# A mixture-of-experts kernel: first gather ahead of two weight loads, first tables ahead of the splits, the overflow branch behind the last expert

## The chip, the cores and the metric

The kernel runs on one core of a Trainium2 chip. The metric is the device time of one execution in microseconds, as the median of several runs. Beside those runs there is one profiled execution, with a trace of every instruction. All times of the trace count from the start of its span. The engines are PE (TensorE: matmuls and transposes), DVE (VectorE), ACT (ScalarE), POOL (GpSimd) and SP (SyncE, which here only issues DMAs). Each engine runs its own list of instructions strictly in that list's order.

## What is computed

The reference is a model of two layers on 512 tokens of width 1024. The part that this case is about is the mixture of experts at the end of the first layer: a router picks 4 of 32 experts for each token, and each expert is a clamped SwiGLU.

```python
def moe(h, w_router, b_router, w_gu, b_gu, w_down, b_down):
    """Top-4-of-32 clamped SwiGLU experts; tokens sorted by expert into expert-homogeneous blocks."""
    ...
    logits = (xt @ w_router + b_router).astype(jnp.float32)
    top_vals, top_idx = lax.top_k(logits, TOP_K)
    ...
```

An expert's gate and up weights are 1024 x 2048 and its down weights 1024 x 1024, all float32. The first layer's mixer (gated linear attention and pooling) runs ahead of this, and the second layer follows it: a short Fourier mixing of 128 x 256 pieces, attention with keys and values, and a dense feed-forward part.

## The kernel before, in words

`phase_a` is the first layer up to the router. `phase_b` (L1070 on) is the mixture of experts, and `phase_c` the second layer. Only `phase_b` is changed.

**Experts.** Each expert has a block of 96 slots (`SLOTS`). `gather(e)` (L1092) is an indirect DMA that POOL issues: it fetches the 96 token rows of expert e from `h2d`, in DRAM, into `xg`. `turn` (L1098) transposes them on PE (`pxT`) and splits the result into two parts, `xTh` (a rounded copy, on ACT) and `xTl` (the rest, on DVE). `gate_up(e)` (L1123) runs over 8 slabs of 128 x 2048 weights, `swiglu` (L1138) makes `g` and `u` from its PSUM (L1142 to L1145), `turn` makes `aTh` and `aTl` of them, and `down(e)` (L1148) runs over 4 slabs of the down weights and ends in `y` (L1162) and a scatter with accumulation into `ydr` (L1163), again by POOL. In the program `down(e-1)` stands behind `gate_up(e)`, so PE has the down of the expert before to do while `g` and `u` are made.

**Weights.** `W.get` (L204; its work is in `split`, L147 and L148) takes one slab of 1 MB: it is loaded into one of 9 raw buffers, ACT casts it to `whi`, and DVE subtracts to get `wlo`. One slab feeds 12 matmuls with 512 columns: `whi` with the rounded rows, `wlo` with the rounded rows, `whi` with the rest. There are 4 pairs of `whi` and `wlo`. Seven raw slabs are loaded ahead of the mixture of experts through SP's queue and two more (`ahead[SH:AH]`) through POOL's queue. `held` are the first three splits, written ahead of the loop.

**Tables.** `tables(b)` (L933) makes the row numbers, scatter numbers and weights of four experts: four comparisons `oh` on DVE (L940), 16 small matmuls `ptab` (L944), and some ten small operations on DVE. `tables(0)` stands ahead of the loop, and each further one is called in the gate and up part of every fourth expert. The first gather does not need it; it has its numbers `gi0` from the router.

**Further blocks.** `overflows` (L958) counts the blocks beyond the first of each expert and loads the count into a register of every engine. `overflow` (L976) is a branch, `tc.If(n > 0)`, with a loop over such blocks (L983). With the data here no expert has more than 96 rows, and the branch is skipped.

**What sets the order.** The kernel is written as a program in one order, and a scheduler makes of it a list for each engine, ready instructions first as it judges, within the dependences. A branch is a wall for it: nothing is moved across it. In `order`'s rows below a name is the tile that is written, then `<-`, then the tiles that are read.

Of the kernel before, what the change touches and what calls it, by code (L numbers as in the profile page):

```python
# [29 lines left out]
AH, SH, HN = 9, 7, 3  # L30
# [902 lines left out]
def tables(S, pl, bank, b):  # L933

    nc = S.nc
    es = slice(b * 4, b * 4 + 4)
    oh = pl.tile([128, NT, 4, SLOTS], BF, name="oh", tag="oh", bufs=1)
    iota = S.k[:, None, K_IOTA:K_IOTA + SLOTS].to_broadcast([128, 4, SLOTS])
    for i in range(NT):
        nc.vector.tensor_tensor(oh[:, i], iota, S.pos[:, i, es, None].to_broadcast([128, 4, SLOTS]), op=OP.is_equal)  # L940
    p = bank("ptab")
    for e in range(4):
        for i in range(NT):
            nc.tensor.matmul(p[:SLOTS, e * 6:e * 6 + 6], oh[:, i, e, :], S.V[:, i, b * 4 + e, :], start=i == 0, stop=i == NT - 1)  # L944
    sl = pl.tile([SLOTS, 4, 6], F32, name="sl", tag="sl", bufs=2)
    nc.vector.tensor_copy(sl, p[:SLOTS, 0:24].rearrange("p (e c) -> p e c", e=4))
    t = pl.tile([SLOTS, 4, 4], F32, name="tsl", tag="tsl", bufs=2)
    tok, sct = t[:, :, 0], t[:, :, 1]
    nc.vector.tensor_tensor(tok, sl[:, :, 0], sl[:, :, 1], op=OP.add)
    nc.vector.tensor_copy(S.gi[:, es], tok)  # L950

    nc.vector.scalar_tensor_tensor(sct, sl[:, :, 2], S.k[:SLOTS, K_NSLOT:K_NSLOT + 1], tok, op0=OP.mult, op1=OP.add)
    nc.vector.tensor_scalar(S.si[:, es], sct, S.k[:SLOTS, K_SLOT:K_SLOT + 1], None, op0=OP.add)
    nc.vector.tensor_tensor(sct, sl[:, :, 3], sl[:, :, 4], op=OP.add)
    nc.vector.tensor_tensor(S.wt[:, es], sct, sl[:, :, 5], op=OP.add)
# [114 lines left out]
def phase_b(S):  # L1070
    nc, tc, I = S.nc, S.tc, S.I
    mm = nc.tensor.matmul
    with ExitStack() as bx:
# [4 lines left out]
        W = Weights(S, bx, 2048, 9, "b_w", (2, 3, 0, 1, 4, 5, 8, 6, 7))  # L1078
        W.open_parts(bx, 4, "b_wp", (0, 1, 2, 3, 4, 7, 6, 5))
        pl = bx.enter_context(tc.tile_pool(name="b_pool", bufs=1, reuse_waits="tile"))  # L1080
# [11 lines left out]
        def gather(e, gi=None):  # L1092
            xg[e] = pl.tile([SLOTS, D], F32, name="xg", tag="xg", bufs=2)
            gi = S.gi[:, e:e + 1] if gi is None else gi
            S.gathered = nc.gpsimd.indirect_dma_start(out=xg[e], out_offset=None, in_=S.h2d,
                                         in_offset=bass.IndirectOffsetOnAxis(ap=gi, axis=0)).ins

        def turn(src, dst, e, name, bufs, scale=1.0):  # L1098
            dst[e] = [pl.tile([128, KT, SLOTS], F32R, name=name + n, tag=name + n, bufs=bufs) for n in "hl"]
            for h in range(2):  # L1100
                p = bank("p" + name)
                for k in range(4):
                    kk = h * 4 + k
                    nc.tensor.transpose(p[:, k * SLOTS:(k + 1) * SLOTS], src[:, kk * 128:(kk + 1) * 128], S.ident[:SLOTS, :SLOTS])  # L1104
                hi, lo = [t[:, h * 4:h * 4 + 4, :] for t in dst[e]]
                p = p[:, :4 * SLOTS].rearrange("p (k t) -> p k t", k=4)
                if scale == 1.0:
                    split(S, hi, lo, p)
                else:
                    nc.scalar.mul(hi, p, scale)  # L1110
                    nc.vector.scalar_tensor_tensor(lo, p, scale, hi.bitcast(F32), op0=OP.mult, op1=OP.subtract)
# [61 lines left out]
                nc.sync.dma_start(br[64 + h:96 + h, 0:512], bgu[:, 1536:2048])  # L1173
                nc.sync.dma_start(br[64 + h:96 + h, 512:1536], bdn)
        S.ahead = W.last

        with tc.issue_after(S.h2d_last):
            W.ahead(ahead[SH:AH], [128, 2048], nc.gpsimd)
        nc.vector.tensor_copy(sel.rearrange("p h e -> p (h e)"), S.k[:, K_SEL:K_SEL + 64])
        gather(0, S.gi0)  # L1180
        with tc.issue_after(S.gathered):
            nc.gpsimd.dma_start(S.g2b, bcast(S.adr, D, off=3 * D, parts=SLOTS))
        with tc.issue_after(S.gathered):
            overflows(S, pl)
        overflow(S, pl, ps, bank, W)
        held = [W.get(I["w_gu"][0, 0, k * 128:(k + 1) * 128, :], [128, 2048]) for k in range(HN)]
        tables(S, pl, bank, 0)
        gather(1)
        turn(xg.pop(0), xT, 0, "xT", 2)
        for e in range(NE + 1):  # L1190
            if e < NE:
                between = {BK: biases} if e == 0 else {}
                if e % 4 == 0 and e // 4 + 1 < NE // 4:
                    between[TK] = lambda: tables(S, pl, bank, e // 4 + 1)
                if e + 1 < NE:
                    between[XK] = lambda: turn(xg.pop(e + 1), xT, e + 1, "xT", 2)
                p = gate_up(e, between)
                ac[e] = swiglu(e, p)
                if e == 6:
                    vectors(S, pl, bank)  # L1200
                if e + 2 < NE:
                    gather(e + 2)
            if e > 0:
                down(e - 1)
            if e < NE:
                turn(ac.pop(e), aT, e, "aT", 1, 1.0 / ALPHA)


def turned(S, pl, bank, xT, i, xn):
# [710 lines left out]
```

## Time and profile before

| what | value |
|---|---|
| median of 3 runs | 2286.84 us (2286.39 to 2287.12) |
| profiled execution | 2284.15 us |
| its span in the trace | 2282.4 us |
| PE busy | 2163.1 us, 95% of the span |
| DVE busy | 1802.1 us, 79% |
| ACT busy | 1335.7 us, 59% |
| POOL busy | 339.2 us, 15% |
| mean rate of all DMAs | 246 GB/s over the span |

The profiled execution is 2.69 us below the median of the runs, and 1.75 us longer than its span. The share of busy time is an average over stages. The mixture of experts takes the stretch from about 322 us to 1533 us, and the second layer what is behind it. In the rows further down, a number in brackets at a row's end is the time the engine stood idle just ahead of that row, and behind the arrow stands what it waited for.

### The profile page before, as it was taken

Reading aid. Unit: us, or ns where it says so; the run is one execution under the profiler, and the core shown is the slowest. Engines: PE = TensorE matmul, PEld = TensorE weight load, DVE = VectorE, ACT = ScalarE, POOL = GpSimd, SP = SyncE. Lnnn points to the kernel's source line nnn. Section 1 sums busy time; section 2 is a strip of 40 time slices with the busy share of each in tenths; the row PEclk is TensorE's granted clock in tenths of the full one; section 3 lists DMA queues with packets and bytes.
Section 4 is the critical chain, followed back from the end, with each engine's and each line's share of the span. In section 5 each row is a group of like instructions: output and inputs, shape, how many; then the busy total and the mean of one; then the engine's idle time right before and its main releaser. Section 6 shows DMA issues by size and latency. Waiting matters only on the chain.

```text
span 2282.4 us, 27718 instructions
## 1 busy us (share of the span) xinstructions
PE 2163.1 (95%) x10501; PEld 1626.5 (71%) x10501; DVE 1802.1 (79%) x2000; ACT 1335.7 (59%) x1487; POOL 339.2 (15%) x186
## 2 busy tenths in 40 slices
PE   7998879999999999999999999989999999999998
PEld 3787666777766666666666666667777888878776
DVE  3748789999989898988898989876478454689885
ACT  3434346767766666666666667655354443388872
POOL 3202210100112121312221212151000000000000
PEclk9899989999999999999999999999999999999999
DMA  7644568999999999999999999966311234323222
GB/s 256 200 148 135 221 234 314 370 371 364 369 349 350 361 346 368 341 369 347 361 348 363 344 370 354 350 229 223 102 47 53 79 118 139 121 74 92 93 83 93
DMA packets 158049, 561.98 MB, mean 246 GB/s; under 512 B 12964, under 2 KB 55304, under 8 KB 125128
## 3 DMA queue, kind: packets, MB, share of 16 engines
q1 hardware_dynamic: 146880, 522.37, 62.3%
q0 software_dynamic: 9968, 36.10, 5.9%
q10 hardware_dynamic: 1064, 1.70, 0.3%
q8 instruction: 84, 1.38, 0.2%
q14 instruction: 53, 0.43, 0.1%
HBM read 534.94 MB, written 25.58 MB: 246 GB/s over the span
## 4 chain that ended last, share of the span: by engine, by line
PE 80%; DVE 11%; DMA 3%; issue 3%; ACT 2%; POOL 1%; SPq 0%; POOLq 0%; DVEq 0%; ACTq 0%
PE pgu L1132 31%; PE pd L1159 12%; DVE wlo L148 3%; PE pjf L153 3%; PE pjf L155 3%; PE pjf L154 3%; PE pop L155 2%; PE pop L153 2%; PE pop L154 2%; DVE u L1144 1%; PE pgu L1115 1%; PE pada L272 1%; DMA ydr<-y,si 1%; PE pxT L1104 1%; PE paT L1104 1%
## 5 line engine op out<-in xcount | busy, mean ns | idle before, releaser
L148 DVE TENSOR_TENSOR wlo<-raw,whi 128x2048 fp32r<-128x2048 f32 (+2 forms) x498 | 1002.5, 2040 | 102.7 <-ACT whi L147 84.2
L147 ACT CAST whi<-raw 128x2048 fp32r<-128x2048 f32 (+2 forms) x454 | 790.6, 1777 | 180.7 <-PE pgu L1132 85.4
L1163 POOL DMA_INDIRECT ydr<-y,si x32 | 185.6, 5801 | 808.8 <-DVE y L1162 777.4
L1132 PE MATMUL pgu<-whi,xTh 128*96 128x512 f32 x1024 | 281.2, 396 | 2.6 <-DVE u L1144 2.6
L1132 PE MATMUL pgu<-wlo,xTh 128*96 128x512 f32 x1024 | 278.5, 394 | 0.3 <-DVE wlo L148 0.3
L1132 PE MATMUL pgu<-whi,xTl 128*96 128x512 f32 x1024 | 278.5, 394 | 0.0
L1132 PEld LDWEIGHTS pgu<-wlo,xTh 128*96 128x96 f32 x1024 | 165.2, 162 | 70.8 <-DVE wlo L148 0.7
L1132 PEld LDWEIGHTS pgu<-whi,xTl 128*96 128x96 f32 x1024 | 165.3, 162 | 69.8 <-issue 0.5
L1132 PEld LDWEIGHTS pgu<-whi,xTh 128*96 128x96 f32 x1024 | 161.7, 162 | 70.2 <-issue 3.2
L1159 PE MATMUL pd<-wlo,aTh 128*96 128x512 f32 x512 | 162.4, 398 | 32.5 <-DVE wlo L148 32.5
L153 PE MATMUL pjf<-xTh,whi 128*128 128x512 f32 (+1 forms) x480 | 181.7, 379 | 1.5 <-DVE rsq L221 1.5
L155 PE MATMUL pjf<-xTh,wlo 128*128 128x512 f32 (+1 forms) x480 | 180.9, 378 | 2.1 <-DVE wlo L148 2.1
L154 PE MATMUL pjf<-xTl,whi 128*128 128x512 f32 (+1 forms) x480 | 180.5, 376 | 0.0
L1159 PE MATMUL pd<-whi,aTh 128*96 128x512 f32 x512 | 159.6, 393 | 0.0
L1159 PE MATMUL pd<-whi,aTl 128*96 128x512 f32 x512 | 159.3, 392 | 0.0
L1159 PEld LDWEIGHTS pd<-wlo,aTh 128*96 128x96 f32 x512 | 79.0, 161 | 72.3 <-DVE wlo L148 43.2
L1143 ACT ACTIVATE g<-g 96x1024 f32<-96x1024 f32 x32 | 33.9, 1060 | 137.0 <-DVE g L1142 137.0
L1159 PEld LDWEIGHTS pd<-whi,aTl 128*96 128x96 f32 x512 | 82.3, 161 | 35.5
L1159 PEld LDWEIGHTS pd<-whi,aTh 128*96 128x96 f32 x512 | 82.3, 161 | 35.4
L155 PEld LDWEIGHTS pjf<-xTh,wlo 128*128 128x128 f32 x480 | 90.3, 188 | 19.2 <-DVE wlo L148 2.9
L153 PEld LDWEIGHTS pjf<-xTh,whi 128*128 128x128 f32 x480 | 90.4, 188 | 17.8 <-ACT jkr L1485 1.4
L154 PEld LDWEIGHTS pjf<-xTl,whi 128*128 128x128 f32 x480 | 90.4, 188 | 16.3
(541 smaller groups left out, 3542.2 us busy)
## 6 DMA issues: line engine op xcount, KB each, us to landing
raw<-in_w_gu_dram SPq DMA_DIRECT2D x254, 1024.0 KB, 9.2
raw<-in_w_down_dram SPq DMA_DIRECT2D x128, 1024.0 KB, 7.0
raw<-in_w_ada_dram SPq DMA_DIRECT2D x40, 512.0 KB, 4.6
raw<-in_even_w_in_dram SPq DMA_DIRECT2D x36, 512.0 KB, 3.5
raw<-in_odd_w_in_dram SPq DMA_DIRECT2D x32, 512.0 KB, 3.8
raw<-in_even_w_out_dram SPq DMA_DIRECT2D x16, 512.0 KB, 3.3
raw<-in_odd_w_out_dram SPq DMA_DIRECT2D x16, 512.0 KB, 3.1
raw<-in_w_in_dram SPq DMA_DIRECT2D x14, 512.0 KB, 4.7
```

The source lines that it names most:

```text
L147: S.nc.scalar.copy(hi, src)
L148: S.nc.vector.tensor_tensor(lo, src, hi.bitcast(F32), op=OP.subtract)
L153: mm(ps, lh, rh, start=start, stop=False)
L154: mm(ps, lh, rl, start=False, stop=False)
L155: mm(ps, ll, rh, start=False, stop=stop)
L272: mm(p[n][q * 32:(q + 1) * 32, :], ada[:, j, :], w[:, n, :], start=j < 4, stop=j >= 4)
L1104: nc.tensor.transpose(p[:, k * SLOTS:(k + 1) * SLOTS], src[:, kk * 128:(kk + 1) * 128], S.ident[:SLOTS, :SLOTS])
L1115: mm(p[:, c * 512:(c + 1) * 512], lhs, bt[:, b % 3 * 512:(b % 3 + 1) * 512], start=start, stop=stop)
L1132: mm(p[:, c * 512:(c + 1) * 512], a[:, k, :], w[:, c * 512:(c + 1) * 512], start=k == 0 and w is wh and a is xh, stop=False)
L1143: nc.scalar.activation(g, g, AF.Silu, scale=ALPHA)
L1159: mm(p[:, c * 512:(c + 1) * 512], a[:, k0 + k, :], w[:, k, c * 512:(c + 1) * 512], start=False, stop=k0 + k == KT - 1 and a is al)
L1163: nc.gpsimd.indirect_dma_start(out=S.ydr, out_offset=bass.IndirectOffsetOnAxis(ap=S.si[:, e:e + 1], axis=0), in_=y, in_offset=None, comput ...
```

## The change

It has three parts, all in `phase_b`. The first gather is issued by POOL ahead of the two weight loads on POOL's queue, which now wait for it in the order. `tables(0)` is written ahead of the three splits of `held`. `overflow`, with its branch and the pair of weight buffers that it borrows, is written behind the loop over the experts.

```diff
         S.ahead = W.last
-
-        with tc.issue_after(S.h2d_last):
-            W.ahead(ahead[SH:AH], [128, 2048], nc.gpsimd)
         nc.vector.tensor_copy(sel.rearrange("p h e -> p (h e)"), S.k[:, K_SEL:K_SEL + 64])
         gather(0, S.gi0)
+        with tc.issue_after(S.gathered):
+            W.ahead(ahead[SH:AH], [128, 2048], nc.gpsimd)
         with tc.issue_after(S.gathered):
             nc.gpsimd.dma_start(S.g2b, bcast(S.adr, D, off=3 * D, parts=SLOTS))
         with tc.issue_after(S.gathered):
             overflows(S, pl)
-        overflow(S, pl, ps, bank, W)
+        tables(S, pl, bank, 0)
         held = [W.get(I["w_gu"][0, 0, k * 128:(k + 1) * 128, :], [128, 2048]) for k in range(HN)]
-        tables(S, pl, bank, 0)
         gather(1)
         turn(xg.pop(0), xT, 0, "xT", 2)
...
             if e < NE:
                 turn(ac.pop(e), aT, e, "aT", 1, 1.0 / ALPHA)
+        overflow(S, pl, ps, bank, W)
```

The scheduler's lists change with it far beyond these lines. Three places follow.

**DVE at the start.** This is DVE's list behind the small operations of the router, before. `ox` and `oni` belong to `overflows`; L983 is the branch.

```order
L964 SCALAR_TENSOR_TENSOR ox<-cnt,ox 128x32 x4
L966 TENSOR_TENSOR_SCAN ox<-ox 128x32
L968 CAST oni<-ox 1x1
L148 TENSOR_TENSOR wlo<-raw,whi 128x2048 x3
L971 TENSOR_LOAD oni
L983 COMPARE_AND_BRANCH x2
...
L940 TENSOR_TENSOR oh<-cst_k,pos 128x384 x4
L148 TENSOR_TENSOR wlo<-raw,whi 128x2048
L946 COPY sl<-ptab 96x24
L148 TENSOR_TENSOR xTl<-pxT,xTh 128x384
```

And the same place now:

```order
L968 CAST oni<-ox 1x1
L946 COPY sl<-ptab 96x24
L940 TENSOR_TENSOR oh<-cst_k,pos 128x384
L949 TENSOR_TENSOR tsl<-sl 96x4
L940 TENSOR_TENSOR oh<-cst_k,pos 128x384
L950 CAST gi<-tsl 96x4
L952 SCALAR_TENSOR_TENSOR tsl<-sl,cst_k,tsl 96x4
L148 TENSOR_TENSOR xTl<-pxT,xTh 128x384
L953 TENSOR_SCALAR si<-tsl,cst_k 96x4
L148 TENSOR_TENSOR xTl<-pxT,xTh 128x384
L954 TENSOR_TENSOR tsl<-sl 96x4
L940 TENSOR_TENSOR oh<-cst_k,pos 128x384
```

Before, three `wlo` stand ahead of the branch and so ahead of the gathered rows' `xTl`, and a fourth follows ahead of it. Now no `wlo` stands ahead of `xTl`; comparisons of the first and second tables do.

**DVE around expert 4's `g`.** `pd` is the down part of expert 3, and the numbers tell the buffers apart. This is DVE before, and below it now; the `wlo` that expert 3's down reads are 4173, 4191, 4209 and 4227 before, and 4011, 4029, 4047 and 4065 now.

```order
L148 TENSOR_TENSOR wlo_4173<-raw_4170,whi_4172 128x2048
L148 TENSOR_TENSOR xTl_4086<-pxT_4087,xTh_4085 128x384
L148 TENSOR_TENSOR xTl_4086<-pxT_4094,xTh_4085 128x384
...
L148 TENSOR_TENSOR wlo_4191<-raw_4188,whi_4190 128x2048
...
L148 TENSOR_TENSOR wlo_4209<-raw_4206,whi_4208 128x2048
L1142 TENSOR_SCALAR g_4159<-pgu_3963 96x1024
L1144 TENSOR_SCALAR u_4160<-pgu_3963 96x1024
L148 TENSOR_TENSOR wlo_4227<-raw_4224,whi_4226 128x2048
```

```order
L148 TENSOR_TENSOR wlo_3978<-raw_3975,whi_3977 128x2048
L148 TENSOR_TENSOR wlo_4011<-raw_4008,whi_4010 128x2048
L1142 TENSOR_SCALAR g_3997<-pgu_3801 96x1024
L1144 TENSOR_SCALAR u_3998<-pgu_3801 96x1024
L148 TENSOR_TENSOR wlo_4029<-raw_4026,whi_4028 128x2048
L1145 SCALAR_TENSOR_TENSOR u_3998<-u_3998,g_3997 96x1024
L148 TENSOR_TENSOR wlo_4047<-raw_4044,whi_4046 128x2048
```

Before, three of the down part's four `wlo` stand ahead of `g` of expert 4; now one does, and the second stands behind `g` and `u`.

**SP behind the last expert.** Before, the loads for the second layer stand in one row; `fw` are the weights of the Fourier mixing.

```order
L197 DMA raw<-in_cst_dch_dram 128x2x512
L1713 DMA fnw<-in_final_norm_w_dram 128x1024
L1714 DMA env<-in_even_norm_dram 128x1024
L1353 DMA fw<-in_fourier_w_dram 128x4x256 x2
L197 DMA raw<-in_even_w_in_dram 128x2x512 x4
L1726 DMA hr<-ydr 128x1024 x4
```

Now (between the two pieces lies the body of the branch, which is skipped):

```order
L1713 DMA env<-in_even_norm_dram 128x1024
L197 DMA raw<-in_even_w_in_dram 128x2x512 x3
L971 TENSOR_LOAD oni
L983 COMPARE_AND_BRANCH x2
...
L1352 DMA fw<-in_fourier_w_dram 128x4x256 x2
L197 DMA raw<-in_even_w_in_dram 128x2x512
L1725 DMA hr<-ydr 128x1024 x4
```

The two loads of `fw` moved behind three of the four `raw` loads and behind the branch. On PE, 95 of the 96 matmuls `pG` that read `fw`'s split stood ahead of the first transposes of the second layer's rows (`pxn`) before, and 55 do now.

## Rows read from the trace of the kernel before

**Rows 1.** The page's part 5: busy time, mean ns, idle before and releaser.

```profile
L1159 PE MATMUL pd<-wlo,aTh 128*96 128x512 f32 x512 | 162.4, 398 | 32.5 <-DVE wlo L148 32.5
```

**Rows 2.** Busy time by stretch, from one expert's g to the next.

```profile
core 0: us, PE busy (x) PEld busy (x) DVE busy (x) ACT busy (x) POOL busy (x), PEclk, DMA share, GB/s
361.66:390.86 29.20, 26.70 (x119) 18.89 (x120) 25.39 (x21) 19.06 (x15) 1.34 (x1) 0.94 0.89 338
...
462.21:498.91 36.70, 36.70 (x184) 26.22 (x183) 35.66 (x33) 25.58 (x18) 3.13 (x2) 1.00 1.01 373
498.91:534.72 35.81, 35.81 (x168) 25.40 (x167) 33.50 (x22) 25.49 (x18) 2.85 (x2) 1.00 1.01 371
570.59:606.14 35.55, 35.55 (x166) 25.21 (x165) 34.41 (x49) 27.03 (x21) 3.82 (x2) 1.00 1.01 376
606.14:642.74 36.60, 36.60 (x183) 26.16 (x182) 35.58 (x31) 24.98 (x17) 7.44 (x2) 1.00 0.98 354
642.74:679.02 36.28, 36.28 (x169) 25.74 (x168) 30.84 (x19) 23.20 (x16) 8.22 (x2) 1.00 0.93 338
679.02:716.49 37.47, 36.06 (x167) 25.34 (x166) 33.04 (x21) 24.89 (x17) 8.21 (x2) 1.00 0.97 354
753.95:792.34 38.39, 36.98 (x183) 26.04 (x182) 35.66 (x31) 24.68 (x17) 10.17 (x2) 1.00 0.97 364
```

**Rows 3.** PE's timeline, 679 to 690 us, around expert 9's g.

```profile
681.58 0.63 PE L1159 MATMUL pd<-whi,aTh 128*96 128x512 f32 x2
683.62 0.71 PE L1159 MATMUL pd<-wlo,aTh 128*96 128x512 f32 x2 [1.41 <-DVE wlo L148]
```

**Rows 4.** DVE's timeline, 675 to 692 us.

```profile
679.02 1.22 DVE L1142 TENSOR_SCALAR g<-pgu 96x1024 f32<-96x1024 f32 x1 [3.42 <-PE pgu L1115]
...
681.29 2.28 DVE L148 TENSOR_TENSOR wlo<-raw,whi 128x2048 fp32r<-128x2048 f32 x1
```

**Rows 5.** The chain of waits, 315 to 340 us: start, duration, what.

```profile
322.93 9.11 DMA xg<-h2d,gi
```

**Rows 6.** DMA issues, 316 to 345 us; chain of waits, 1500 to 1600 us.

```profile
h2d<-h POOLq DMA_DIRECT2D x2, 512.0 KB, 3.5
...
1538.87 5.70 DMA ydr<-y,si
```

**Rows 7.** DVE's timeline, 320 to 364 us: start, duration, what, idle before.

```profile
324.03 6.70 DVE L148 TENSOR_TENSOR wlo<-raw,whi 128x2048 fp32r<-128x2048 f32 x3
330.95 1.97 DVE L940 TENSOR_TENSOR oh<-cst_k,pos 128x384 bf16<-128x384 f32 x4 [0.21 <-DVEq L983]
...
338.50 0.56 DVE L148 TENSOR_TENSOR xTl<-pxT,xTh 128x384 fp32r<-128x384 f32 x1 [2.09 <-ACT xTh L147]
...
340.77 1.75 DVE L1121 TENSOR_TENSOR bt<-br,bt 32x1536 fp32r<-32x1536 f32 x1
...
361.67 1.21 DVE L1142 TENSOR_SCALAR g<-pgu 96x1024 f32<-96x1024 f32 x1
```

**Rows 8.** ACT's timeline, 322 to 340 us.

```profile
322.10 5.50 ACT L147 CAST whi<-raw 128x2048 fp32r<-128x2048 f32 x3 [1.50 <-DMA h2d<-h]
327.84 1.28 ACT L147 ACT_TABLE_LOAD   x1 [0.24 <-ACTq L983]
...
333.13 0.48 ACT L147 CAST xTh<-pxT 128x384 fp32r<-128x384 f32 x1 [2.10 <-PE pxT L1104]
```

**Rows 9.** Timelines of SP's queue, ACT and PE, 1515 to 1545 us.

```profile
1525.39 2.52 SPq L1353 DMA_DIRECT2D fw<-in_fourier_w_dram  x2
...
1534.18 1.05 ACT L147 CAST ws<-fw 128x1024 fp32r<-128x1024 f32 x1 [7.19 <-DMA fw<-in_fourier_w_dram]
...
1535.28 0.50 PE L153 MATMUL pG<-ws,whi 128*128 128x256 f32 x2 [2.23 <-ACT ws L147]
```

**Rows 10.** Busy time by stretch, second layer, columns as before.

```profile
1543.00:1553.60 10.60, 8.65 (x71) 8.21 (x70) 6.77 (x11) 8.06 (x15) 0.73 (x1) 1.00 0.76 262
1553.60:1583.40 29.80, 26.20 (x128) 21.20 (x127) 18.78 (x44) 12.35 (x22) 2.32 (x3) 1.00 0.86 305
```

## The prediction

> **What bounds the kernel now.** I read the page's groups first. PE is busy for 95% of the span. Its idle time in the experts' part sits almost all in one group, the `pd` matmuls that read `wlo`: 32.5 us, all of it spent waiting for DVE's `wlo` [rows 1]. The table of busy time from one expert's `g` to the next shows where that idle time lies. Up to expert 8 a stretch equals PE's busy time (expert 4: 35.81 of 35.81 us). From expert 9 on it is 37.47 us with 36.06 busy, and 38.39 with 36.98 where a table is made (expert 11) [rows 2]. So PE loses 1.41 us in each of the last 23 experts and nothing before.
>
> The two timelines of one such expert say why. PE stops for 1.41 us ahead of the second down slab's first `wlo` matmul [rows 3]. DVE is then doing `g`, `u` and the `wlo` of that slab, which ends at 683.6, 4.6 us after `g` began [rows 4]. Nothing is slow there. The slab's `wlo` merely stands behind `g` and `u` in DVE's list. In what follows, "lead" is the number of down slabs whose `wlo` stands ahead of the `g` in the list. By the list of before it is 3 for experts 0 to 6, 2 for experts 7 and 8, and 1 from expert 9 on: the same boundaries that the stretches show. With a lead of 2 or 3 DVE's `g` and `u` hide behind PE's work; with 1 they cost 1.41 us.
>
> Where does the lead come from? At the start the rows of expert 0 come 9.11 us after the gather's issue [rows 5], and in that wait DVE makes three `wlo` (324.03 to 330.7) [rows 7]. They stand ahead of the branch, which no instruction may cross, so the scheduler had to put them there.
>
> **The change, part by part.** The sum is made against the profiled execution (2284.15 us; its span is 2282.4), which is 2.69 us below the median of the runs.
>
> *Gather first.* Its issue stays where it is, since it waits for its row numbers and for `h2d`. Now no two 1 MB loads are ahead of it on its queue. No row shows such a gather alone. From below I take the 512 KB store to `h2d`, 3.5 us, from above the last scatter, alone on POOL's queue, 5.70 us [rows 6]. It lands at 326.4 to 328.6 instead of 332.0. The Trainium skill, "DMA: Bandwidth & Descriptors", section "Anatomy of one DMA", gives 2.0 us plus bytes over 436 GB/s, so 2.9 us for these 384 KB, an estimate; no run here shows it, and by it the start below would be 0.6 us earlier at best.
>
> *Tables first, and no wall behind the splits.* The early rows buy little, since the splits no longer fill the wait. From the landing to the first `xTl` it is 1.6 us (`xTh` ended at 333.61, the rows had come at 332.04) [rows 5, 8]. From there to expert 0's `g` DVE's list now holds 10 `wlo` of 2.23, 6 `oh` of 0.49, 4 `xTl` of 0.5, 2 `bt` of 1.75 and some ten table operations of 0.12 [rows 7]: 22.3 + 2.9 + 2.0 + 3.5 + 1.2 = 31.9 us, with hardly a gap to spare since `whi` takes 1.83 on ACT [rows 8]. So `g` comes at 359.9 to 362.1, and a few tenths later if the first `wlo` waits for its `whi`. Before it came at 361.67 [rows 7]. I take 0 for the start, with 1.8 us of gain and 1.0 of loss as ends. What the early gather gains, the missing three splits give back.
>
> *The lead.* In the list of now the lead is 2, 3, 2 for experts 0 to 2, 1 for 3, 4 and 5, 0 for expert 6, and 1 from 7 on. Expert 4's place in the change's section shows it. Each stretch is priced by a stretch of before with that lead [rows 2]: expert 2 goes from a lead of 3 (35.81, as expert 4) to 2 (36.28, as expert 8), +0.5; expert 3, with a table, from 36.70 to 38.39, +1.7; experts 4 and 5 from 35.81 to 37.47, +1.7 each; expert 7 from 36.60 to 38.39, +1.8; expert 8 from 36.28 to 37.47, +1.2. Experts 0 and 1 I leave alone. Expert 6 has no row of before. There the small operations for the second layer (`vectors`) pushed one `wlo` back, so PE needs the late `wlo` one slab earlier. A down slab is six pairs of matmuls of 0.46, so 2.76 us: the wait is 1.41 + 2.76 = 4.2, and some 0.5 more for small operations among the next `wlo`, so +4.7 on the 35.55 of before. Sum: 0.5 + 1.7 + 3.4 + 4.7 + 1.8 + 1.2 = 13.3. From expert 9 on the lists agree, so nothing is added and nothing is won back: PE has no slack to catch up in.
>
> *PE's clock behind expert 6.* PE idled 2.6 us in the stretch of expert 0 (29.20 with 26.70 busy), and the granted clock of that stretch was 0.94, while the 1.41 us waits left it at 1.00 [rows 2]. A share of 6% of 29.2 us is 1.75 us. Expert 6's wait is longer than the one that lowered the clock, so I take 1.7, with 0 as the lower end.
>
> *The branch at its old place.* DVE idled 0.21 us and ACT 0.24 plus a table load of 1.28 behind it [rows 7, 8], all while everything waited for the rows. Its removal is worth 0 there.
>
> *The branch at its new place.* SP skips it only after its own earlier loads have landed, and `fw` is now behind it. Before, the two `fw` were issued at 1525.39 and the first `ws` started at 1534.18, 8.8 us later [rows 9]. Now three raw loads, `fnw` and `env` (2.5 MB) must land first. At the 262 GB/s of the stretch that follows [rows 10] that is 9.6 us; `fnw` and `env` were issued about 1 us ahead of `fw`, so `fw` goes out near 1534. `ws` starts behind that by 4 us (the 1 MB of `fw` at that rate) to 8.8 (as before), and `pG` 1.1 us later: 4 to 9 us behind the 1535.28 of before [rows 9]. The rows of `hr` come by the last scatter, which is not moved, so `pxn` starts near 1553.6 as before. Some 41 `pG` no longer fit ahead of it; at 0.107 us each (a 256-column matmul, half of the 0.23 of 512) that is 4.4 us. Up to 3.6 of this can go into PE's idle time behind (29.80 with 26.20 busy) [rows 10], so at least 0.8. I take 2.5.
>
> Sum: 0 + 13.3 + 1.7 + 0 + 2.5 = 17.5. From 2284.15 that is 2301.7, and with the 2.69 to the median of the runs 2304.3. I predict 2304.
>
> **Rivals.** Each time is on the scale of the median, and 0.2% of it is 4.6 us, about what a measurement of this kernel can tell from no change.
>
> *The gather's gain carries through: faster.* PE is the bound, so rows that come 3.5 to 5.6 us earlier move all 32 experts forward, if the lead is only how the list happens to look. For it speaks the 95%. It decides from the point where expert 0's `g` comes before 358 and experts 3 to 8 keep stretches under 36.7. Then 2286.84 - 4.6 = 2282. Against it: DVE's 31.9 us, and that stretches and lead change at the same experts. 3%.
>
> *The lead costs little, and only the second layer pays.* If DVE caught up at a lead of 1, it would be 2.5 us more: 2289. The 23 equal stretches of 37.47 speak against it. 6%.
>
> *The lead alone.* No lower clock, and the `pG` go into idle time (0.8): 2286.84 + 13.3 + 0.8 = 2301; with the early end of the start 2299. 25%.
>
> *The branch stalls.* The old place had waits to hide behind; the new one has PE waiting for ACT and DVE. An engine that has to fetch its instructions anew there could stand longer than the 0.21 to 0.24 us of before [rows 7, 8]; between those and a landing of 3.5 us [rows 6], I take 3: 2307. The Trainium skill, "Runtime: NRT & Kernel Launch", section "Instruction fetch mechanics", says that a taken branch out of the prefetched window stalls for a fetch. The rows of before neither show nor exclude a longer one. 11%.
>
> My forecast has the remaining 55%.
>
> **How the numbers follow.** The range takes in the lead alone with the early start (2299) less 2 us for expert 6 if its wait is shorter, so 2297, and the branch's stall with the start's late end and a microsecond of `pG`, 2309. Faster by over 0.2% is the first rival alone, 0.03; within 0.2% is the second, 0.06; slower the rest, 0.91.
>
> **What would show it.** Right: the gather lands near 327, yet expert 0's `g` stays within 1.5 us of 361.7; the stretches of experts 3, 4, 5, 7 and 8 are 37.5 to 38.4 with PE waiting 1.41 us for `wlo` in each; expert 6 takes about 40 us; from expert 9 on all is as before, 13 to 15 us later; the first `pG` comes 4 to 9 us later behind the last `g`. Wrong: stretches of 35.8 at a lead of 1, an expert 0 that starts 3 us earlier, or a second layer that is longer by more than 5 us.

## The result, and where the profile after differs

The changed kernel takes 2314.74 us (median of 4 runs, 2307.80 to 2316.72), the kernel before 2286.98 us (2286.39 to 2289.26). The ratio is 1.012, with a 95% interval of 1.0099 to 1.014, so the change costs 22.6 to 32.0 us. Forecast were 2304 us and a range up to 2309. The direction was right and the size was not: 17.5 us forecast, 27.8 measured.

The profiled execution of the changed kernel took 2316.72 us, with a span of 2315.0. Against the execution of before that is 32.6 us more. Four marks cut both spans into five pieces: DVE's `sel` (the last instruction ahead of the changed part), the `g` of experts 0, 9 and 31, and the end of the span. They are starts of rows of DVE's timeline, and each piece is a difference of two of them (the last one runs to the end of the span).

| piece, us | before | changed | difference | forecast |
|---|---|---|---|---|
| start of span to `sel` (first layer) | 322.36 | 326.57 | +4.2 | 0 |
| `sel` to `g` of expert 0 (start) | 39.31 | 41.99 | +2.7 | 0 |
| `g` of expert 0 to 9 (lead and clock) | 317.35 | 333.54 | +16.2 | 15.0 |
| `g` of expert 9 to 31 | 827.59 | 830.95 | +3.4 | 0 |
| `g` of expert 31 to the end (second layer) | 775.75 | 781.90 | +6.2 | 2.5 |

The first piece is not the change's. Up to `sel` the engines' lists are the same line for line, and in the profiled executions of this study that piece takes 319.3 to 326.6 us, whatever the kernel. Single runs of the kernel before spread from 2278.17 to 2290.91 us. Without this piece the differences add up to 28.4 us, which agrees with 27.8 of the medians. Each piece comes from one execution, so a microsecond or two in it can be that execution's own; the experiments below show how much.

**The experts.** The page of the changed kernel, part 5, answers to [rows 1]:

```profile
L1159 PE MATMUL pd<-wlo,aTh 128*96 128x512 f32 x512 | 164.7, 403 | 42.6 <-DVE wlo L148 42.6
```

The wait for `wlo` grew from 32.5 to 42.6 us. The busy time by stretch, from one expert's `g` to the next (experts 2, 3, 4, 6, 7, 8, 9 and 11), answers to [rows 2]:

```profile
432.73:469.19 36.46, 36.46 (x169) 25.81 (x168) 30.84 (x20) 23.22 (x16) 8.20 (x2) 1.00 0.90 327
469.19:507.58 38.39, 36.98 (x183) 26.09 (x182) 35.66 (x31) 24.67 (x17) 10.13 (x2) 1.00 0.97 361
507.58:545.22 37.64, 36.23 (x167) 25.40 (x166) 33.04 (x20) 24.91 (x17) 8.21 (x2) 1.00 0.94 343
583.22:626.05 42.83, 38.92 (x167) 26.93 (x168) 37.88 (x44) 28.89 (x20) 4.74 (x2) 0.92 0.93 332
626.05:664.45 38.40, 36.99 (x183) 26.09 (x182) 35.66 (x32) 24.67 (x17) 10.10 (x2) 1.00 0.91 344
664.45:702.10 37.65, 36.24 (x167) 25.40 (x166) 33.04 (x20) 24.90 (x17) 8.21 (x2) 1.00 0.96 341
702.10:739.76 37.66, 36.25 (x167) 25.40 (x166) 33.04 (x20) 24.89 (x17) 8.21 (x2) 1.00 0.96 358
777.42:815.82 38.40, 36.99 (x183) 26.09 (x182) 35.65 (x31) 24.66 (x17) 10.10 (x2) 1.00 0.98 365
```

Experts 3, 4, 7 and 8 now show the pattern that only experts from 9 on had: 36.23 busy in 37.64, 36.98 in 38.39. Expert 6, with a lead of 0, takes 42.83 us, and the granted clock of its stretch is 0.92. PE's timeline there, and the clock of the 4 us that follow the wait:

```profile
584.09 0.70 PE L1159 MATMUL pd<-whi,aTh 128*96 128x512 f32 x2 [1.09 <-ACT whi L147]
587.84 1.17 PE L1159 MATMUL pd<-wlo,aTh 128*96 128x512 f32 x2 [3.04 <-DVE wlo L148]
588.80 1.05 PE L1159 MATMUL pd<-whi,aTl 128*96 128x512 f32 x2
```

```profile
583.22:588.00 4.78, 0.87 (x3) 0.41 (x4) 4.78 (x6) 4.75 (x4) 0.00 (x0) 0.78 0.82 343
588.00:592.00 4.00, 4.00 (x10) 2.65 (x11) 4.00 (x5) 3.80 (x3) 0.00 (x0) 0.50 0.78 260
592.00:600.00 8.00, 8.00 (x39) 5.71 (x39) 7.50 (x13) 3.83 (x2) 0.00 (x0) 0.95 0.95 350
```

PE waits 1.09 us for ACT's `whi` and 3.04 us for DVE's `wlo`, and behind that the granted clock is 0.50, which is 1.2 GHz, for all 4 us of the second stretch.

**The start.** The chain of waits has the gather, and PE's and ACT's timelines what follows it:

```profile
327.00 4.73 DMA xg<-h2d,gi
```

```profile
331.78 1.54 PE L1104 MATMUL pxT<-cst_k,xg 96*128 96x96 f32 x8 [1.22 <-DMA xg<-h2d,gi]
...
335.69 2.02 PE L1132 MATMUL pgu<-whi,xTh 128*96 128x512 f32 x4 [0.43 <-ACT whi L147]
...
355.67 1.17 PE L1132 MATMUL pgu<-whi,xTh 128*96 128x512 f32 x4 [1.01 <-ACT whi L147]
358.41 1.17 PE L1132 MATMUL pgu<-wlo,xTh 128*96 128x512 f32 x4 [1.56 <-DVE wlo L148]
```

```profile
333.73 7.30 ACT L147 CAST whi<-raw 128x2048 fp32r<-128x2048 f32 x4
346.97 0.86 ACT L147 CAST xTh<-pxT 128x384 fp32r<-128x384 f32 x2 [5.94 <-PE pxT L1104]
...
351.92 7.31 ACT L147 CAST whi<-raw 128x2048 fp32r<-128x2048 f32 x4 [2.28 <-PE pgu L1132]
```

The rows come 4.73 us after the issue, where it was 9.11 [rows 5]. The Trainium skill's "DMA: Bandwidth & Descriptors", section "Anatomy of one DMA", would give 2.9 us for these 384 KB, an estimate. The trace has 4.73 us for a gather of 96 rows, and the measurement decides. But ACT's first `whi` now stands behind both `xTh`, at 333.73, 7.2 us behind `sel`. Before, three `whi` were done by 327.6 [rows 8]. PE then waits for `whi` and `wlo` in the middle of expert 0. DVE waits too: from the first `xTl` (333.23) to `g` (368.56) its waits for `whi` and `ptab` add up to 3.6 us.

**The second layer.** The rows that answer to [rows 9] are these of SP's queue and of PE, and the chain of waits:

```profile
1551.71 2.19 SPq L197 DMA_DIRECT2D raw<-in_even_w_in_dram  x3
1565.12 0.93 SPq L1352 DMA_DIRECT2D fw<-in_fourier_w_dram  x2
```

```profile
1570.56 0.79 PE L153 MATMUL pG<-ws,whi 128*128 128x256 f32 x2 [11.10 <-ACT ws L147]
```

```profile
1547.93 16.15 DMA ydr<-y,si
...
1564.82 8.42 DMA ydr<-y,si
1573.26 3.51 DMA hr<-ydr
```

SP issues `fw` 13.4 us behind `raw`, at 1565.12. What it waits for in between is its own earlier loads. The list of SP's waits from 1552 to 1570 us has five at the branch (L983):

```profile
SPq L983 <- SPq L983: 10.1, 5, 3.8
```

The last of them ends at 1564.66, when the third `raw` has landed (last update of its semaphore in the trace: 1564.64). The scatter of expert 30 had landed at 1564.08 (1547.93 + 16.15), which is close, but not what released SP: in the seven kernels with the branch behind the last expert `fw` goes out 0.5 us behind the landing of that `raw`, and 0.64 to 1.36 us behind that of the scatter. From the issue of `fnw` (1550.85) the five loads took 13.8 us to land, with the scatter beside them.

PE stands idle for 11.10 us and not 2.23. The last scatter now takes 8.42 us and not 5.70 [rows 6], while the loads of `fw` run beside it (that they are the reason is argued from the overlap), and `hr`, which reads what it wrote, is issued 40.2 us after the last `g` instead of 38.0.

### The profile page after: what moved, and what is told of

It reads as the page before. It is cut to its first block, busy times and chain, and to the rows that moved or that the text cites. A ratio compares the mean times of both kernels' runs of the same rounds, so it can differ in the third digit from the quotient of the medians.

```text
span 2315.0 us, 27721 instructions
## 1 busy us (share of the span) xinstructions
PE 2179.6 (94%) x10501; PEld 1634.6 (71%) x10501; DVE 1800.0 (78%) x2000; ACT 1329.4 (57%) x1486; POOL 363.5 (16%) x186
## 4 chain that ended last, share of the span: by engine, by line
PE 79%; DVE 11%; issue 3%; DMA 3%; ACT 2%; POOL 1%; POOLq 0%; DVEq 0%; ACTq 0%; SPq 0%
PE pgu L1132 30%; PE pd L1159 11%; DVE wlo L148 4%; PE pjf L154 3%; PE pjf L153 3%; PE pjf L155 3%; PE pop L155 2%; PE pop L153 2%; PE pop L154 2%; DVE u L1144 2%; PE pgu L1115 1%; DMA ydr<-y,si 1%; PE pada L272 1%; PE pxT L1104 1%; PE paT L1104 1%
## 5 line engine op out<-in xcount | busy, mean ns | idle before, releaser
L1163 POOL DMA_INDIRECT ydr<-y,si x32 | 204.9, 6404 | 844.3 <-DVE y L1162 801.4
L1159 PE MATMUL pd<-wlo,aTh 128*96 128x512 f32 x512 | 164.7, 403 | 42.6 <-DVE wlo L148 42.6
L1142 DVE TENSOR_SCALAR g<-pgu 96x1024 f32<-96x1024 f32 x32 | 39.1, 1221 | 87.3 <-PE pgu L1115 87.3
```

What stands on the lines that cost most here:

```text
L1142: nc.vector.tensor_scalar(g, p[:, 0:D], 7.0, None, op0=OP.min)
L1159: mm(p[:, c * 512:(c + 1) * 512], a[:, k0 + k, :], w[:, k, c * 512:(c + 1) * 512], start=False, stop=k0 + k == KT - 1 and a is al)
L1163: nc.gpsimd.indirect_dma_start(out=S.ydr, out_offset=bass.IndirectOffsetOnAxis(ap=S.si[:, e:e + 1], axis=0), in_=y, in_offset=None, comput ...
```

## The experiments

Twelve kernels, each compared with the kernel before on the same chip. The medians of the kernel before in the three groups of runs were 2284.18 us (the first four), 2285.64 (the next four) and 2284.70 (the last four). The table gives the pieces of each profiled execution, worked out as above; g0 is the `g` of expert 0.

| kernel | median us | ratio to before, 95% interval | `sel` to g0 | g0 to g9 | g9 to g31 | g31 to end |
|---|---|---|---|---|---|---|
| before | 2286.98 | | 39.31 | 317.35 | 827.59 | 775.75 |
| changed | 2314.74 | 1.0120 (1.0099 to 1.0140) | 41.99 | 333.54 | 830.95 | 781.90 |
| 1 branch only | 2310.61 | 1.0111 (1.0093 to 1.0129) | 38.29 | 332.51 | 830.93 | 781.89 |
| 2 gather only | 2285.52 | 1.0004 (0.9993 to 1.0016) | 39.67 | 315.83 | 827.62 | 777.43 |
| 3 branch back | 2283.75 | 0.9996 (0.9984 to 1.0008) | 39.60 | 315.82 | 827.99 | 777.01 |
| 4 lead of before | 2299.98 | 1.0068 (1.0051 to 1.0086) | 43.05 | 319.28 | 830.96 | 782.46 |
| 5 pair early | 2314.95 | 1.0130 (1.0104 to 1.0157) | 43.10 | 333.89 | 830.98 | 782.25 |
| 6 gather, lead 3 | 2247.53 | 0.9835 (0.9806 to 0.9865) | 39.76 | 316.94 | 793.26 | 773.52 |
| 7 gather, lead 2 | 2248.08 | 0.9845 (0.9818 to 0.9871) | 39.40 | 316.10 | 792.07 | 775.34 |
| 8 branch in the middle | 2312.68 | 1.0120 (1.0095 to 1.0144) | 41.66 | 333.43 | 836.60 | 775.80 |
| 9 old addresses | 2309.66 | 1.0099 (1.0078 to 1.0119) | 42.30 | 333.20 | 828.17 | 783.76 |
| 10 splits first | 2312.65 | 1.0111 (1.0087 to 1.0135) | 40.24 | 331.67 | 830.99 | 783.42 |
| 11 three undone | 2295.66 | 1.0043 (1.0027 to 1.0060) | 39.88 | 318.78 | 828.23 | 783.54 |
| 12 lead 3 alone | 2248.64 | 0.9826 (0.9803 to 0.9849) | 40.08 | 317.00 | 792.69 | 774.03 |

### 1, 2 and 3: one part at a time

The first moves nothing but the branch:

```diff
-        overflow(S, pl, ps, bank, W)
         held = [W.get(I["w_gu"][0, 0, k * 128:(k + 1) * 128, :], [128, 2048]) for k in range(HN)]
...
                 turn(ac.pop(e), aT, e, "aT", 1, 1.0 / ALPHA)
+        overflow(S, pl, ps, bank, W)
```

> The kernel before with only the branch moved behind the last expert; gather, loads, splits and tables stand in their old order. DVE's list has the same lead of the down slabs as the changed kernel's (2, 3, 2, 1, 1, 1, 0, then 1). Theory (the branch was the wall that kept three splits ahead, and the lost lead is the bulk of the loss): +13 to +16 us over experts 2 to 8, +2 to +6 us behind the last expert, and nothing won at the start, so 2303 to 2315 us. Rival (the order on POOL's queue or the tables ahead of the splits make the loss): within 5 us of the kernel before, 2282 to 2292 us.

It took 2310.61 us, and its trace has 332.51 us from expert 0 to 9 and the second layer's 781.89. Against the kernel before in its own group of runs that is 26.4 us, so one part carries nearly the whole loss. The stretch of expert 4 shows the lost lead without any other part of the change:

```profile
503.25:540.88 37.63, 36.22 (x167) 25.40 (x166) 33.04 (x20) 24.91 (x17) 8.21 (x2) 1.00 0.96 346
```

The second takes only the gather's move:

```diff
-        with tc.issue_after(S.h2d_last):
-            W.ahead(ahead[SH:AH], [128, 2048], nc.gpsimd)
         nc.vector.tensor_copy(sel.rearrange("p h e -> p (h e)"), S.k[:, K_SEL:K_SEL + 64])
         gather(0, S.gi0)
+        with tc.issue_after(S.gathered):
+            W.ahead(ahead[SH:AH], [128, 2048], nc.gpsimd)
```

> The kernel before with only the first gather ahead of the two loads on POOL's queue. The lead is that of before (3, then 2, 2, then 1). Theory: the rows land 4.5 to 5 us after their issue and not 9.1, no stretch of an expert is longer, and expert 0's g comes 2 to 4 us earlier: 2283 to 2286 us. Rival (the two loads come too late for the slabs that need them): slabs 7 and 8 make ACT wait, and the time is 2290 us or more.

It is no faster: 2285.52 us, ratio 1.0004 (0.9993 to 1.0016). The expectation of 2 to 4 us at the start failed, and the trace says why. The view of `xg` has 5.0 us as its shortest landing, so the rows were there by 325.1 (issue at 320.04). PE's first instruction of this part still waits for DVE:

```profile
328.69 0.24 PE L944 MATMUL ptab<-V,oh 128*96 128x6 bf16 x1 [10.00 <-DVE oh L940]
328.79 0.56 PE L1104 MATMUL pxT<-cst_k,xg 96*128 96x96 f32 x2
```

```profile
321.17 6.70 DVE L148 TENSOR_TENSOR wlo<-raw,whi 128x2048 fp32r<-128x2048 f32 x3
328.07 1.96 DVE L940 TENSOR_TENSOR oh<-cst_k,pos 128x384 bf16<-128x384 f32 x4 [0.21 <-DVEq L983]
```

DVE makes its three `wlo` and passes the branch first, until 328.07, 8.5 us behind `sel`. The gather's 9.11 us of before were hidden behind this, but for some tenths.

Its g0 to g9 is 1.5 us shorter than before (315.83 and 317.35), though the lists of all engines are the same but for the gather's place on POOL. Nearly all of it is in the stretch of expert 0, which answers to the first line of [rows 2]:

```profile
359.28:387.02 27.74, 25.25 (x120) 18.04 (x121) 25.36 (x21) 19.22 (x15) 1.31 (x1) 1.00 0.96 365
```

PE idles 2.5 us here as it did before (27.74 less 25.25, and 29.20 less 26.70), but the granted clock is 1.00 and not 0.94. The third, sixth, seventh and twelfth kernel, with the same list up to there, have 1.00 too. So the lower clock of [rows 2] belongs to that execution, and not to every wait of this length.

The third is the change with the branch put back ahead of the tables, so gather and tables stay first:

```diff
+        overflow(S, pl, ps, bank, W)
         tables(S, pl, bank, 0)
         held = [W.get(I["w_gu"][0, 0, k * 128:(k + 1) * 128, :], [128, 2048]) for k in range(HN)]
...
-        overflow(S, pl, ps, bank, W)
```

> The changed kernel with the branch back ahead of the tables and splits (gather first and tables first stay). The lead in DVE's list is that of before. Theory: no loss over experts 2 to 8 and none behind the last expert; 2282 to 2289 us. Rival (tables ahead of the splits are a good part of the loss): 2295 us or more.

2283.75 us, ratio 0.9996 (0.9984 to 1.0008): what the change does beside the branch neither costs nor gains anything that can be measured while the wall stands. The scheduler's lists are the second kernel's line for line, so the 1.8 us between the two medians is what the same lists can differ by. With the branch moved, the place of `tables(0)` has no effect at all: with the splits written first again, the lists of all engines are the same line for line as the changed kernel's. So the gather's move alone separates the first kernel from the changed one. With the wall gone the start is longer with it, 41.99 us against 38.29. The early rows let the scheduler put `xTh` and `xTl` ahead of the splits; the tenth kernel shows what that is worth, 1.75 us. Beside the order PE's clock differs: from 12 to 17 us behind `sel` the granted clock is 0.50 in the changed and in the tenth kernel and 1.00 in the first. What the clock is worth of the other 1.95 us no run separates.

### 4: the lead of before, in the changed kernel

The down slabs that should stand ahead of `g` are split in the program ahead of `swiglu`, and `g` is queued behind their last `wlo`:

```diff
                 p = gate_up(e, between)
-                ac[e] = swiglu(e, p)
+                n = (0, 3, 3, 3, 3, 3, 3, 2, 2)[e] if e < 9 else 0
+                if n:
+                    first += [slab(e - 1, k0) for k0 in range(0, 2 * n, 2)]
+                    with tc.issue_after(S.lo):
+                        ac[e] = swiglu(e, p)
+                else:
+                    ac[e] = swiglu(e, p)
```

> The changed kernel, with the list of before restored at one point: for experts 1 to 8 as many down slabs are split ahead of g as in the kernel before (3, for 7 and 8 two). Branch, gather and tables stay where the change put them. Theory: the stretches of experts 2 to 8 go back to 35.5 to 36.7 us, so 13 to 16 us less than the changed kernel: 2298 to 2303 us. Rival (the loss sits in the start, the matmuls' rate and the end): it stays above 2308 us.

2299.98 us, 14.8 less than the changed kernel's median (11.9 by the two ratios, since the medians are of different groups of runs), and g0 to g9 takes 319.28 us, 14.3 less. Experts 4 and 6, and 9 with its lead of 1:

```profile
503.57:537.24 33.67, 33.67 (x158) 23.89 (x157) 33.04 (x21) 25.01 (x17) 4.28 (x2) 1.00 1.00 365
573.23:609.52 36.29, 36.29 (x169) 25.32 (x168) 34.76 (x49) 27.81 (x21) 6.98 (x2) 1.00 1.02 391
681.64:719.29 37.65, 36.23 (x167) 25.44 (x166) 33.04 (x20) 24.90 (x17) 8.21 (x2) 1.00 0.96 355
```

PE is busy for all of the first two stretches, at a clock of 1.00, and waits in the third. (Tables fall on other sides of the marks here, so expert 4 has 33.67 us.) The lead is shown as the cause of this term.

### 5 and 9: why each later stretch is 0.17 us longer

From expert 9 on the lists agree, yet a stretch takes 37.66 us with 36.25 busy and not 37.47 with 36.06 [rows 2]. PE does not wait longer; each matmul is slower. Two matmuls of `pgu` that follow each other in one group start 0.2303 us apart and not 0.2294 (mean of 384 pairs in 16 stretches, `wlo` with `xTh`). The fifth kernel takes the borrowed pair of buffers ahead of the splits, so that each slab has its old buffers:

```diff
-    ow = [t.bitcast(F32) for t in W.pair()]
+    ow = [t.bitcast(F32) for t in S.ow]
...
+        S.ow = W.pair()
         tables(S, pl, bank, 0)
```

> The changed kernel, where the pair of buffers that the branch borrows is taken ahead of the first splits, as in the kernel before; every slab then has the same whi and wlo buffer as before. Asked: why a stretch without a table takes 37.63 us from expert 9 on in the changed kernel and 37.47 before, though the lists agree (3.4 us over experts 9 to 31). Theory (the shift by one pair of buffers): the stretches are 37.47 us again and experts 9 to 31 take 827.6 us. Rival (the branch's place itself): 37.63 us and 831 us stay.

Nothing changed: 830.98 us. That theory fell. The built programs differ in one more thing. The branch's small tiles were allotted first, and are allotted last now, so that `xTh`, `xTl`, `aTh` and `aTl`, which the matmuls read, and `g`, `u` and `y` stand at other SBUF addresses (`aTh`: 217440 before, 208704 now, bytes in a partition). The ninth kernel allots the branch's tiles at the old point. No instruction of the experts' part moves with it (in the second layer one split of a weight does):

```diff
+        places(S, pl)
         tables(S, pl, bank, 0)
...
+def places(S, pl):
+    o = S.ot = {}
+    o['le'] = pl.tile([128, 2, NE], F32, name="ole")
...
+    pl.tile([128, KT, SLOTS], F32, name="oxTh", tag="xTh", bufs=2)
+    pl.tile([SLOTS, D], F32, name="g", tag="g", bufs=1)
...
```

> The changed kernel, where the small tiles of the branch are allotted ahead of the tables, as before; with that xTh, xTl, aTh, aTl, g, u and y stand at the SBUF addresses that they had before, and no instruction is moved. Asked again: why a stretch without a table takes 37.63 us from expert 9 on in every kernel with the moved branch, with the pair shifted or not. Theory (the addresses of the tiles, which moved because the branch's tiles are now allotted last): 37.47 us again, experts 9 to 31 take 827.6 us and the whole is 3 to 4 us below the changed kernel, 2310 to 2312 us. Rival (the code's own place or another cause): 37.63 and 831 us stay.

828.17 us, the matmuls start 0.2294 us apart again, and the stretches of experts 4 and 9 have PE's old busy time. The fifth kernel's expert 9 and the ninth's experts 4 and 9:

```profile
701.43:739.07 37.64, 36.23 (x167) 25.45 (x166) 33.03 (x20) 24.90 (x17) 8.21 (x2) 1.00 0.97 356
```

```profile
504.58:542.04 37.46, 36.05 (x167) 25.34 (x166) 33.05 (x21) 24.91 (x17) 8.21 (x2) 1.00 0.96 343
697.69:735.18 37.49, 36.08 (x167) 25.34 (x166) 33.04 (x20) 24.91 (x17) 8.21 (x2) 1.00 0.98 354
```

The addresses are shown as the cause of 2.8 us of the 3.4 in the piece from expert 9 to 31, and the eleventh kernel repeats it (828.23). Which of these tiles it is, and why an address matters, stays open.

### 8: the wall behind expert 15

```diff
                 turn(ac.pop(e), aT, e, "aT", 1, 1.0 / ALPHA)
-        overflow(S, pl, ps, bank, W)
+            if e == 15:
+                overflow(S, pl, ps, bank, W)
```

> The changed kernel with the branch behind expert 15 and not behind the last. DVE's list has the changed kernel's lead up to expert 15, then 3 and 2 for experts 16 and 17, then 1. Theory (the branch as a wall behind the last expert costs the second layer 6 us by holding back its loads): from the last g to the end it takes 776 us as before and not 782, and about 2 us come back in experts 16 and 17; the wall's own cost in the middle is 0 to 4 us: 2303 to 2311 us against the changed kernel's 2314.7. Rival (the second layer is slower for another reason, its own list): 782 us stay.

The second layer is back at 775.80 us. Its first `pG` comes after 2.15 us of idle time, and the last scatter takes 5.43 us:

```profile
1564.64 0.50 PE L153 MATMUL pG<-ws,whi 128*128 128x256 f32 x2 [2.15 <-ACT ws L147]
```

```profile
1568.31 5.43 DMA ydr<-y,si
```

So the branch's place behind the last expert costs the second layer its 6 us. But in the middle the wall costs more than expected. The stretch of expert 15, and PE's wait in it:

```profile
926.00:973.98 47.98, 39.80 (x183) 27.72 (x182) 42.43 (x37) 28.67 (x19) 8.69 (x3) 0.89 0.90 325
973.98:1009.50 35.52, 35.52 (x165) 25.18 (x164) 31.16 (x21) 24.19 (x17) 2.79 (x2) 1.00 0.96 344
```

```profile
946.14 1.99 PE L1132 MATMUL pgu<-whi,xTh 128*96 128x512 f32 x4 [6.76 <-DVEq L983]
```

47.98 us are 9.6 more than the 38.39 of a table's stretch. PE waits 6.76 us for DVE to pass the branch, and the granted clock of the stretch is 0.89. Behind the wall the lead is 3 and 2 for two experts, and the first of them takes 35.52. The total, 2312.68 us, is 2 below the changed kernel and above the upper end that was expected.

### 10: the splits first

```diff
-        tables(S, pl, bank, 0)
         held = [W.get(I["w_gu"][0, 0, k * 128:(k + 1) * 128, :], [128, 2048]) for k in range(HN)]
+        lo = S.lo
+        with tc.issue_after(lo):
+            tables(S, pl, bank, 0)
         gather(1)
-        turn(xg.pop(0), xT, 0, "xT", 2)
+        with tc.issue_after(lo):
+            turn(xg.pop(0), xT, 0, "xT", 2)
```

> The changed kernel, with DVE's list at the start forced to the order of before: the three splits ahead of the first comparisons and of xTl. Theory (without the wall the scheduler put the early rows' work ahead of the splits, and the splits' lateness costs the start): from sel to expert 0's g it takes 38 to 40 us and not 42.0; the rest stays, so 2 to 4 us below the changed kernel, 2310 to 2313 us. Rival (the later loads on POOL's queue delay the start): 42 us stay.

40.24 us from `sel` to `g` of expert 0, just above the 38 to 40 expected, and 1.75 of the changed kernel's 2.7 come back. By expert 9 it is another 1.9 us less, but 1.5 of that is expert 0's stretch with a clock of 1.00 and not 0.94 (27.65 us, 29.12 in the changed kernel), which differs between executions of the same list as the second kernel shows. The second layer of this execution took 783.42 us. The total, 2312.65, is 2 us below the changed kernel, which the spread of the runs does not tell from nothing; the piece carries this reading.

### 11: three of four undone

The edits of 4, 9 and 10 together, with the branch still behind the last expert.

> The changed kernel with three of its four losses undone at once: the lead of before for experts 1 to 8, the old addresses, and the three splits first. The branch is still behind the last expert. Theory (four separate terms: about 14 to 16 us lead, 3.4 addresses, 3 start, 6 second layer): only the second layer's 6 us are left, 2287 to 2294 us against 2285 of the kernel before. Rival (a further term is hidden among them): 2297 us or more.

2295.66 us, ratio 1.0043 (1.0027 to 1.0060): 11.0 us are left against the kernel before in the same group of runs, of 27.8. The pieces add up to 10.4 us more than before (0.6, 1.4, 0.6 and 7.8). It missed the 2287 to 2294 expected by 1.7 us. Most of it is the second layer, with 7.8 us and not 6.2. In the ninth and the tenth kernel it lost as much (8.0 and 7.7). The kernel before, 2, 3 and 8, with the branch ahead of the last expert, have 775.75 to 777.43 us there, so 1.7 us are the spread of this piece. Why it is 6.1 to 6.7 us in the changed kernel, 1, 4 and 5 and up to 8.0 in these stays open.

### 6, 7 and 12: a lead for every expert

The same experiment that restores the lead can give it to all experts. The sixth kernel has three slabs ahead of `g` from expert 1 on, with the gather first; the seventh has two from expert 7 on (its edit asks for two everywhere, and in the list a third stands ahead for experts 1 to 6); the twelfth has three, with nothing of the change.

```diff
-                ac[e] = swiglu(e, p)
+                n = 3 if e else 0
+                if n:
+                    first += [slab(e - 1, k0) for k0 in range(0, 2 * n, 2)]
+                    with tc.issue_after(S.lo):
+                        ac[e] = swiglu(e, p)
```

> The kernel with the gather first alone, and in it three down slabs are split ahead of g for every expert from the second on, written into the program. Theory (the lead sets each stretch): all stretches are 35.5 to 36.7 us with PE never waiting for wlo, 1.4 to 1.6 us less in each of 23 experts and 0.4 in two, so 33 to 37 us less than the kernel before: 2249 to 2254 us. Rival (the loads are the next bound, since the DMA engines are busy 97 to 100% of the time): stretches of 36.3 us or more, 2262 us or more.

> As the run with three slabs ahead of g, but with two from expert 7 on. Theory: expert 8 of the kernel before has a lead of two and takes 36.3 us without a wait of PE, so this is as fast as three within 5 us, 2249 to 2258 us. Rival (two leave a short wait in each): 10 us or more behind three.

> The kernel before, with nothing of the change, and three down slabs split ahead of g for every expert from the second on. Theory (the gain of 38 us is all of the lead): within 4 us of the same kernel with the gather first, 2244 to 2252 us. Rival (the earlier gather is worth something once the lead is kept): 5 us or more behind it.

They take 2247.53, 2248.08 and 2248.64 us, 1.5 to 1.7% below the kernel before; the first two are 1 to 1.5 us below the low end expected. Part 5 of the page of the sixth kernel, its experts 9 and 10, and experts 9 and 10 of the twelfth:

```profile
L1163 PE MATMUL pd<-wlo,aTh 128*96 128x512 f32 x512 | 159.2, 392 | 0.0
```

```profile
681.68:717.52 35.84, 35.84 (x167) 25.39 (x166) 33.03 (x22) 25.12 (x17) 4.29 (x2) 1.00 1.00 369
717.52:753.44 35.92, 35.92 (x168) 25.42 (x167) 33.03 (x21) 25.11 (x17) 4.29 (x2) 1.00 1.00 369
```

```profile
682.03:717.83 35.80, 35.80 (x168) 25.39 (x167) 33.04 (x21) 25.11 (x17) 4.29 (x2) 1.00 1.00 377
717.83:753.63 35.80, 35.80 (x168) 25.39 (x167) 33.04 (x21) 25.11 (x17) 4.29 (x2) 1.00 1.01 370
```

PE's wait for `wlo` went from 32.5 us to 0.0. The DMA engines are busy all the time (1.00), and PE is busy for all of these stretches, so the rival of a bound by loads, 36.3 us or more, is refuted at this rate. Two slabs do as well as three within the spread of the runs. The gather adds nothing that can be measured, as in the second kernel. These three beat both kernels of the case.

The sixth kernel's last scatter also bears on the second layer. It takes as long as in the changed kernel, with the two `fw` issued 9 and 7 us ahead of it:

```profile
1500.29 8.35 DMA ydr<-y,si
```

The two `fw` and three `raw` land during it and a fourth just behind (the twelfth kernel is alike, 8.40 us). So a long scatter goes with loads in flight beside it, and late `fw` are not the only way to that. How many loads, and which, was not tested.

## Why the prediction was wrong

The lead held, as mechanism and nearly in size. Four terms of the sum did not.

- *The lead* was forecast at 13.3 us and the clock behind expert 6 at 1.7, together 15.0; measured 16.2, and 14.3 came back in the same piece of the fourth kernel. Experts 3, 4, 7 and 8 came at 38.39, 37.64, 38.40 and 37.65 against 38.39, 37.47, 38.39 and 37.47 forecast. In expert 6 PE's waits add up to the 4.2 us forecast (1.09 + 3.04 = 4.1), but the 1.09 for ACT's `whi` was not in the forecast, so part of that is luck. Its stretch grew by 7.3 us, not by 4.7 and 1.7: PE was busy for 3.4 us more than before, with the clock at 0.92 of full. The clock's 1.7 had been priced from expert 0's stretch, whose 0.94 the same list shows in one execution and not in the next. For expert 0 the prediction also names leads (3 and 2); no down part stands ahead of its `g`, and no sum used them.
- *The start*, the step that said "What the early gather gains, the missing three splits give back", was forecast at 0, between 1.8 of gain and 1.0 of loss; measured +2.7. The count of DVE's work was right, but it was summed "with hardly a gap to spare", and DVE waited 3.6 us. ACT's first `whi` stood behind both `xTh`, and one `whi` out of turn waited for PE to free its buffers. In the tenth kernel, which forces the old order, 1.75 us came back. That a kept wall would have hidden the gather's gain altogether, the second kernel showed; the prediction did not see it.
- *"From expert 9 on the lists agree, so nothing is added"* failed: +3.4 us, of which the ninth kernel returned 2.8. Equal lists do not make equal times when the tiles moved.
- *The branch at its new place* was the largest miss: 2.5 us forecast, 6.2 measured. That SP waits there for its own earlier loads was right. Their price was wrong: 9.6 us at the 262 GB/s of a later stretch, 13.8 us measured, so `fw` went out 32.1 us after the last `g` and not near 27.4. The trace of before had a nearer row: there `fnw`, `env` and the two `fw`, half a megabyte each, took 12.8 us from the first issue (1524.41) until ACT's wait for the second `fw` ended (1537.24). And "The rows of `hr` come by the last scatter, which is not moved" was wrong in its size: the scatter started in its place, 31.8 us after the last `g` (32.3 before), but took 8.42 us and not 5.70, and `pxn` began 50.6 us after the last `g` and not 46.5. The first `pG` came 8.8 us later, inside the 4 to 9 forecast, but by two errors against each other: `fw` left 4.7 us late, and `ws` followed it by 4.3 us, near the lower of the two ends. The price of a `pG`, 0.107 us, is not half of 0.23, which is 0.115; the 4.4 us would then be 4.7.

The misses (1.2, 2.7, 3.4 and 3.7 us) all went one way, and the range had no room for three small terms at once. The rivals with a faster kernel, or with a loss in the second layer alone, were refuted by the first and the fourth kernel. The rival of a branch that stalls did not come as it was put. Where an engine stood long at the branch, the trace names another end of its wait: SP's own loads behind the last expert, DVE's earlier splits in the middle (6.76 us of PE). The rule of the Trainium skill on taken branches ("Runtime: NRT & Kernel Launch", "Instruction fetch mechanics") is not shown by any run here.

## What to carry to other kernels

A branch or any other barrier to a scheduler decides the order of everything around it, far beyond its own cost. Here it was worth 26 us by its place alone. Some 15 of them came from the experts 1 to 8: the wall had forced three splits early, and these kept two vector operations of each expert hidden behind PE's work. The rest were mostly loads that it held back in the second layer, and addresses that moved with it. Compare the built lists for the one quantity that the bound engine lives on (here: how many slabs are ready ahead of `g`), and if it matters, write it into the program and don't leave it to chance; that was worth 36 to 38 us. And before moving work off a wait, look for what else ends at the same moment.

## What the runs showed of the hardware that was not expected

The same matmuls, in the same order, ran 0.4% slower (0.2303 against 0.2294 us from one to the next) when `xTh`, `aTh` and the other small tiles of the experts stood at other SBUF addresses, and the old addresses brought the old rate back. PE's clock did not follow from the length of a wait alone: waits of 1.41 us left it at 1.00 in all 23 stretches; the wait of 2.5 us in expert 0 went with 0.94 in the kernel before and with 1.00 in five others with the same list; and expert 6's waits of 1.09 and 3.04 us went with 0.92 in the changed kernel and with 0.96 in the first. A scatter of 96 rows took 5.4 to 5.8 us in the kernel before and in 2, 3, 7 and 8, and 7.2 to 8.5 us in the others, where `fw` was issued within 0.6 us of it or six loads were still landing when it began.
